# Coefficients of a gated linear recurrence from Ln, Exp and one Newton step, on 512 columns, in place of a Sqrt and a reciprocal on 256

## The chip, the cores and the metric

The kernel runs on one core of a Trainium2 chip. The metric is the device time in microseconds (us) of one execution. Before the change it is 1085.87 us, the median of three runs (1085.77 to 1085.95). Five engines work side by side, each through its own queue of instructions in a fixed order, and wait for each other through semaphores: PE (matrix products; its weight loads are listed apart as PEld), DVE (VectorE), ACT (ScalarE), POOL (GpSimd) and SP, which here only issues transfers.

## The reference, cut to what matters

One decoder layer for 256 tokens of width 2048 in float32: a normalisation, one combined projection into six groups of 1024 channels, two parallel groups of heads, an output projection, and a gated feed-forward part with 5632 hidden channels. The change concerns group A, the gated recurrence (RG-LRU) over 1024 channels:

```python
r = sigmoid(einsum(u_blocks, wa) + ba)
i = sigmoid(einsum(u_blocks, wx) + bx)
log_a = LRU_C * r * log_sigmoid(lam)          # LRU_C = 8
a = exp(log_a)
b = sqrt(-expm1(2.0 * log_a)) * (i * u)
h[t] = a[t] * h[t-1] + b[t]                   # a scan over the 256 tokens
y_lru = h * gelu(lru_gate)
```

With t = tanh(-log_a / 2) both coefficients are rational in t and its root: a = (1 - t) / (1 + t), and sqrt(1 - a*a) = 2 sqrt(t) / (1 + t).

## The kernel before, in words

**Layout.** In the first part activations lie with channels on the 128 partitions and tokens along the free dimension; 256 tokens of one block of 128 channels are a tile of 128x256, and two blocks share one tile of 128x512. The eight blocks of the recurrence are n = 0 to 7, so the lists `tt` (t), `iu` (i times u), `root` and `hs` (the scan's result) hold four tiles of 128x512 each, and `pair(lst, n, name)` is the half that belongs to block n.

**Weights.** All weights stream from memory in loads of 128x1024 (512 KB) into one of six `raw` buffers, issued by SP in the order of the program. Each load is split into a high and a low part, so that products in the faster 32-bit format keep their accuracy: `split` casts `wh<-raw` on ACT (L112) and subtracts `wl<-raw,wh` on DVE (L113). There are four `wh` and four `wl` buffers. A cast for load M therefore waits until PE has read load M-4 for the last time, and PE can run at most three loads ahead of what ACT and DVE are doing now.

**The program.** It is a list of steps; each step is a unit of weights with its matrix products (`fm_tile` for tiles with channels on the partitions, `tm_block` for tiles with tokens there). A step of `fm_tile` uses one unit of two loads: for each pair of weight blocks two products with `wh` (L184, 512 columns) and two with `wl` (L186, 256 columns). The casts and subtractions of a load are written into the program three loads ahead of the step that uses them. Work on ACT, DVE and POOL that follows a product is deferred by a number of steps (`defer`). From this program a scheduler with a model of time of its own makes the final order in each engine's queue, so the queues need not follow the text, and a change of one stage may shift the order around it.

**The stages.** v (first half) to 29 us; the projections lx of the recurrence, then k and q (24 steps of `fm_tile`), to about 169 us; v (second half) and ret_gate (`tm_block`), with the heads of the retention between; lg, the recurrence's output gate, to about 292 us; then the output projection and the feed-forward part to the end.

**The recurrence.** `lru_in` (convolution) and `lru_gate` follow the lx steps. `lru_gate(n)` runs two sigmoids and a tanh on ACT (L372, L373, L375), a lower bound on t on DVE (L376), and i times u on POOL (L377). All eight gates done, `lru_roots` takes four square roots of 128x512 on ACT (L384), which needs another table of functions (an ACT_TABLE_LOAD). Then eight times `lru_scan(n)`: seven DVE operations on 128x256 (L390 to L397), one of them a reciprocal (L391), one square on ACT (L394), and the scan itself on DVE (L398). They are deferred by 12 to 28 steps and so lie among the k, q, v and ret_gate steps, whose casts, subtractions and copies use the same queues. The results `hs` are first read in the lg stage, by `lru_out`.

Of the kernel before, what the change touches and what calls it, by code (L numbers as in the profile page):

```python
# [8 lines left out]
F32 = mybir.dt.float32  # L9
F32R = mybir.dt.float32r  # L10
AF = mybir.ActivationFunctionType
ALU = mybir.AluOpType
PSUM = bass.MemoryType.PSUM

P = 128
D = 2048
S = 256
# [3 lines left out]
NLRU = 8  # L21
NH = 8
EPS = 1e-6
TINY = 1e-30


C_LN1, C_LN2, C_CW, C_CB, C_BA, C_BX, C_LAM, C_GN = 0, 16, 32, 64, 72, 80, 88, 96
# [17 lines left out]
def tile_hymba_layer(ctx: ExitStack, tc: tile.TileContext, A: dict, out: bass.AP):  # L45
    nc = tc.nc
    v, act, pool, pe = nc.vector, nc.scalar, nc.gpsimd, nc.tensor

    cpool = ctx.enter_context(tc.tile_pool(name="consts", bufs=1))
# [13 lines left out]
    def nm(s):  # L63
        counter[0] += 1
        return f"{s}_{counter[0]}"

    def act_tile(name, dt=F32):
        return apool.tile([P, 512], dt, tag="act", name=nm(name))
# [7 lines left out]
    def tmp(name):  # L76
        return tpool.tile([P, S], F32, tag="tmp", name=nm(name))
# [4 lines left out]
    def aux(name):  # L82
        return paux.tile([P, 512], F32, tag="aux", name=nm(name))
# [11 lines left out]
    ones = cpool.tile([P, P], F32, name="ones")  # L95
    eps_t = cpool.tile([P, 1], F32, name="eps_t")
    v.memset(ones, 1.0)
    v.memset(eps_t, EPS)
    warm = cpool.tile([P, 1], F32, name="warm")
    act.activation(out=warm, in_=eps_t, func=AF.Tanh)  # L100

# [5 lines left out]
    def col(c):  # L107
        return small[:, c : c + 1]
# [42 lines left out]
    def mm_fm1(ps, wh, wl, hl, first, last):  # L151

        pe.matmul(ps, wh, hl[:, :S], start=first, stop=False)
        pe.matmul(ps, wh, hl[:, S:], start=False, stop=False)
        pe.matmul(ps, wl, hl[:, :S], start=False, stop=last)
# [17 lines left out]
    def fm_tile(unit, acts, order, post, room=bank):  # L173


        def run():
            ps = room("fm")
            for n in range(0, len(order), 2):
                if n == 8 and halfway:
                    halfway.pop()()  # L180

                two = [(*unit.part(k, P, 0, P), acts[k]) for k in order[n : n + 2]]
                for i, (wh, _, hl) in enumerate(two):
                    pe.matmul(ps, wh, hl, start=n + i == 0, stop=False)  # L184
                for i, (_, wl, hl) in enumerate(two):
                    pe.matmul(ps[:, :S], wl, hl[:, :S], start=False, stop=n + i == len(order) - 1)  # L186
            post(ps)

        program.append(([unit], run))

    def tm_block(units, acts, post, together=1, split=()):


# [36 lines left out]
    def defer(steps, f):  # L230
        later.append([steps, f])
# [73 lines left out]
    c2 = cpool.tile([P, NLRU], F32, name="c2")  # L305
    xcs = [None] * NLRU
    xc = [None] * 4
    tt = [None] * 4
    iu = [None] * 4
    hs = [None] * 4  # L310

    def pair(lst, n, name):
        if lst[n // 2] is None:
            lst[n // 2] = act_tile(name)
        return lst[n // 2][:, (n % 2) * S : (n % 2) * S + S]
# [34 lines left out]
    def lru_in(n, ps):  # L350
        xe = epool.tile([P, 260], F32, tag="xe", name=nm("xe"))
        pool.memset(xe[:, 0:3], 0.0)
        t = tmp("lx")
        halves(ps, t)
        v.tensor_tensor(out=xe[:, 3 : 3 + S], in0=t, in1=r1, op=ALU.mult)
        c = pair(xc, n, "xc")
        act.activation(out=c, in_=xe[:, 0:S], func=AF.Identity, scale=col(C_CW + n), bias=col(C_CB + n))
        for tap in range(1, 4):
            v.scalar_tensor_tensor(
                out=c, in0=xe[:, tap : tap + S], scalar=col(C_CW + 8 * tap + n), in1=c, op0=ALU.mult, op1=ALU.add  # L360
            )
        xcs[n] = act_tile("xcs", F32R)
        split(xcs[n][:, :S], xcs[n][:, S:], c)

    def lru_gate(n):
        c = pair(xc, n, "xc")
        ps = aux("gate")
        for g in range(2):
            wh, wl = (w[:, (n % 2) * 256 + g * P : (n % 2) * 256 + g * P + P] for w in gw[n // 2])
            mm_fm1(ps[:, g * S : g * S + S], wh, wl, xcs[n], True, True)  # L370
        r, i = tmp("r"), tmp("i")
        act.activation(out=r, in_=ps[:, :S], func=AF.Sigmoid, bias=col(C_BA + n))  # L372
        act.activation(out=i, in_=ps[:, S:], func=AF.Sigmoid, bias=col(C_BX + n))  # L373
        t = pair(tt, n, "tt")
        act.activation(out=t, in_=r, func=AF.Tanh, scale=c2[:, n : n + 1])  # L375
        v.tensor_scalar(out=t, in0=t, scalar1=TINY, scalar2=None, op0=ALU.max)  # L376
        pool.tensor_tensor(out=pair(iu, n, "iu"), in0=i, in1=c, op=ALU.mult)  # L377

    root = [None] * 4

    def lru_roots():
        for i in range(4):
            root[i] = act_tile("root")
            act.activation(out=root[i], in_=tt[i], func=AF.Sqrt)  # L384

    def lru_scan(n):

        t, s = pair(tt, n, "tt"), pair(root, n, "root")
        p, a, b = tmp("p"), tmp("a"), tmp("b")
        v.scalar_tensor_tensor(out=p, in0=t, scalar=1.0, in1=s, op0=ALU.add, op1=ALU.mult)  # L390
        v.reciprocal(out=p, in_=p)  # L391
        v.scalar_tensor_tensor(out=a, in0=t, scalar=1.0, in1=s, op0=ALU.subtract, op1=ALU.mult)
        v.scalar_tensor_tensor(out=a, in0=a, scalar=-1.0, in1=p, op0=ALU.mult, op1=ALU.mult)
        act.activation(out=b, in_=s, func=AF.Square)  # L394
        v.tensor_tensor(out=b, in0=b, in1=t, op=ALU.add)
        v.tensor_tensor(out=b, in0=b, in1=p, op=ALU.mult)
        v.tensor_tensor(out=b, in0=b, in1=pair(iu, n, "iu"), op=ALU.mult)  # L397
        v.tensor_tensor_scan(out=pair(hs, n, "hs"), data0=a, data1=b, initial=0.0, op0=ALU.mult, op1=ALU.add)  # L398

    y, yf = [None] * (KT // 2), [None] * (KT // 2)  # L400

# [619 lines left out]
    for n in range(NLRU):  # L1021

        def post(ps, n=n):
            defer(max(1, 4 - n), lambda: lru_in(n, ps))
            defer(max(9, 12 - n), lambda: lru_gate(n))
            if n == NLRU - 1:
                defer(10, lru_roots)
                for m in range(NLRU):
                    defer((12, 15, 18, 20, 22, 24, 26, 28)[m], lambda m=m: lru_scan(m))

        fm_tile(Unit(A["w_lx"][n]), u, range(KT), post, room=aux if n in (2, 3, 6, 7) else bank)

# [169 lines left out]
```

## Time and profile before

| | |
|---|---|
| median of three runs | 1085.87 us |
| the profiled execution: its span, first to last instruction | 1084.4 us |
| PE busy | 1074.2 us (99% of the span) |
| DVE busy | 953.5 us (88%) |
| ACT busy | 660.9 us (61%) |
| POOL busy | 51.0 us (5%) |
| granted clock of TensorE | 0.999 |

The profile records the span only; the runs' time is 1.5 us longer, which lies outside the first and the last instruction. Busy shares are averages over stages with different limits, and a busy PE is not by that alone a PE at its peak. What matters for a change of ACT and DVE work is how far these two run ahead of PE in the stage concerned.

### The profile page before, as it was taken

The page shows a single profiled execution, that of the slowest core. Times are in us where ns is not written, and L with a number is a line of the kernel's source. Part 1 is how long each engine was busy: PE and PEld are TensorE (multiplying, and loading weights), DVE is VectorE, ACT ScalarE, POOL GpSimd, SP SyncE. Part 2 cuts the span into 40 slices and gives each one's busy share as a digit, 9 for nine tenths or more (in the row PEclk, how much of TensorE's full clock was granted, in tenths as well). Part 3 has the DMA queues.
Part 4 walks back from the last instruction along what each step waited for, and adds up shares of the span by engine and source line. Part 5 has one row for each costly group of instructions (what it writes and reads, how often), then busy time and mean ns, then how long its engine had stood idle before and what let it go on. Part 6 is the DMA issues. An engine that isn't in the chain of part 4 may idle for free.

```text
span 1084.4 us, 14584 instructions
## 1 busy us (share of the span) xinstructions
PE 1074.2 (99%) x5101; PEld 899.5 (83%) x5101; DVE 953.5 (88%) x1371; ACT 660.9 (61%) x935; POOL 51.0 (5%) x61
## 2 busy tenths in 40 slices
PE   9999999999999999999999999999999999999997
PEld 7888888888888788888888888888888888888885
DVE  7789799988878889888998998999899899898986
ACT  7666644468746676565566566556556666655563
POOL 0612230000000000000000000000000000000001
PEclk9999999999999999999999999999999999999999
DMA  9964474444565567577677677686675756465652
GB/s 330 333 211 168 160 252 173 174 175 171 181 230 205 184 228 275 198 248 266 220 245 261 220 264 235 233 289 214 233 271 194 265 181 213 171 214 199 212 209 85
DMA packets 69274, 238.32 MB, mean 220 GB/s; under 512 B 7888, under 2 KB 8272, under 8 KB 69200
## 3 DMA queue, kind: packets, MB, share of 16 engines
q1 hardware_dynamic: 68400, 235.29, 62.7%
q0 software_dynamic: 512, 1.57, 0.4%
q8 instruction: 40, 0.66, 0.2%
q10 hardware_dynamic: 288, 0.52, 0.1%
q14 instruction: 34, 0.28, 0.1%
HBM read 235.26 MB, written 2.10 MB: 219 GB/s over the span
## 4 chain that ended last, share of the span: by engine, by line
PE 97%; DVE 1%; issue 1%; DMA 0%; ACT 0%; POOL 0%; SPq 0%; POOLq 0%; ACTq 0%
PE c L670 22%; PE c L672 22%; PE c L671 22%; PE fm L184 11%; PE fm L186 5%; PE tm L164 3%; PE tm L165 3%; PE tm L166 3%; PE p L672 1%; PE p L671 1%; PE p L670 1%; PE ft L833 1%; DMA raw<-in_w_v 0%; PE ht L576 0%; PE sc L482 0%
## 5 line engine op out<-in xcount | busy, mean ns | idle before, releaser
L112 ACT CAST wh<-raw 128x1024 fp32r<-128x1024 f32 (+1 forms) x490 | 460.9, 965 | 362.6 <-PE c L672 132.5
L113 DVE TENSOR_TENSOR wl<-raw,wh 128x1024 fp32r<-128x1024 f32 (+1 forms) x490 | 538.2, 1122 | 91.2 <-ACT wh L112 88.4
L671 PE MATMUL c<-wl,ah 128*128 128x512 f32 x850 | 331.0, 390 | 0.0
L672 PE MATMUL c<-wh,al 128*128 128x512 f32 x850 | 330.4, 389 | 0.0
L670 PE MATMUL c<-wh,ah 128*128 128x512 f32 x850 | 275.0, 391 | 0.2 <-ACT wh L112 0.2
L670 PEld LDWEIGHTS c<-wh,ah 128*128 128x128 f32 x850 | 159.4, 188 | 33.4 <-ACT wh L112 1.1
L672 PEld LDWEIGHTS c<-wh,al 128*128 128x128 f32 x850 | 159.6, 188 | 33.0
L671 PEld LDWEIGHTS c<-wl,ah 128*128 128x128 f32 x850 | 159.6, 188 | 32.7
L184 PE MATMUL fm<-u,wh 128*128 128x512 f32 x512 | 161.3, 396 | 0.0
L186 PEld LDWEIGHTS fm<-u,wl 128*128 128x128 f32 x512 | 96.0, 188 | 22.5
L186 PE MATMUL fm<-u,wl 128*128 128x256 f32 x512 | 101.1, 278 | 0.0
L184 PEld LDWEIGHTS fm<-u,wh 128*128 128x128 f32 x512 | 78.4, 189 | 0.3
L648 DVE TENSOR_TENSOR raw<-raw,raw 128x512 f32<-128x512 f32 x106 | 73.1, 690 | 2.8
L648 DVE TENSOR_TENSOR raw<-raw 128x512 f32<-128x512 f32 x106 | 72.7, 689 | 2.4
L671 PE MATMUL c<-wl,sh 128*128 128x512 f32 x176 | 68.5, 389 | 0.0
L672 PE MATMUL c<-wh,sl 128*128 128x512 f32 x176 | 68.0, 389 | 0.0
L670 PE MATMUL c<-wh,sh 128*128 128x512 f32 x176 | 60.4, 394 | 0.3 <-ACT sh L112 0.3
L165 PE MATMUL tm<-wl,u 128*128 128x512 f32 x128 | 48.8, 394 | 0.0
L166 PE MATMUL tm<-wh,u 128*128 128x512 f32 x128 | 48.7, 390 | 0.0
L164 PE MATMUL tm<-wh,u 128*128 128x512 f32 x128 | 47.3, 398 | 0.8 <-ACT u L288 0.8
L954 POOL TENSOR_TENSOR htok<-htok,fw 128x512 f32<-128x512 f32 x2 | 2.5, 1273 | 895.9 <-ACT junk L947 895.9
L670 PEld LDWEIGHTS c<-wh,sh 128*128 128x128 f32 x176 | 33.1, 188 | 7.3 <-ACT sh L112 0.7
(245 smaller groups left out, 1034.9 us busy)
## 6 DMA issues: line engine op xcount, KB each, us to landing
raw<-in_w_gu SPq DMA_DIRECT2D x212, 512.0 KB, 5.5
raw<-in_w_down SPq DMA_DIRECT2D x91, 512.0 KB, 4.3
raw<-in_w_out SPq DMA_DIRECT2D x34, 512.0 KB, 3.7
raw<-in_w_lx SPq DMA_DIRECT2D x16, 512.0 KB, 6.3
raw<-in_w_k SPq DMA_DIRECT2D x16, 512.0 KB, 3.5
raw<-in_w_q SPq DMA_DIRECT2D x16, 512.0 KB, 4.0
raw<-in_w_rg SPq DMA_DIRECT2D x16, 512.0 KB, 3.4
raw<-in_w_lg SPq DMA_DIRECT2D x16, 512.0 KB, 3.4
```

The source lines that it names most:

```text
L112: act.copy(out=dst_h, in_=src)
L113: v.tensor_tensor(out=dst_l, in0=src, in1=dst_h.bitcast(F32), op=ALU.subtract)
L164: pe.matmul(ps, ah, wh, start=first, stop=False)
L165: pe.matmul(ps, ah, wl, start=False, stop=False)
L166: pe.matmul(ps, al, wh, start=False, stop=last)
L184: pe.matmul(ps, wh, hl, start=n + i == 0, stop=False)
L186: pe.matmul(ps[:, :S], wl, hl[:, :S], start=False, stop=n + i == len(order) - 1)
L648: v.tensor_tensor(out=dst, in0=a, in1=b, op=ALU.add)
L670: pe.matmul(p, ah, bh, start=first, stop=False, skip_group_check=onto)
L671: pe.matmul(p, ah, bl, start=False, stop=False, skip_group_check=onto)
L672: pe.matmul(p, al, bh, start=False, stop=last, skip_group_check=onto)
L833: pe.transpose(pt[:, o : o + P], g[:, (2 * b + c) * P : (2 * b + c) * P + P], ident)
```

## The change

`lru_gate` no longer bounds t from below on DVE, and i times u moves from POOL to DVE. `lru_roots` computes, for each of the four pairs, two first guesses on ACT: Ln of (t + 2^-60) and Exp of -0.5 times that for 1/sqrt(t), and Ln of (t + 1) and Exp of minus that for 1/(1 + t). These are 16 activations on 128x512 instead of four. `lru_scan` now works on a pair at once: seven DVE operations on 128x512 and two copies with scale and bias on ACT give one Newton step for each guess and the two coefficients, and two scans of 128x256 follow. There are four such scans instead of eight, deferred by 12, 16, 20 and 24 steps. No reciprocal and no square is left in it. Matrix products, transfers and their numbers stay as they are.

```diff
-TINY = 1e-30
+TINY = 2.0**-60
...
+    tiny_t = cpool.tile([P, 1], F32, name="tiny_t")
+    v.memset(tiny_t, TINY)
...
-        t = pair(tt, n, "tt")
-        act.activation(out=t, in_=r, func=AF.Tanh, scale=c2[:, n : n + 1])
-        v.tensor_scalar(out=t, in0=t, scalar1=TINY, scalar2=None, op0=ALU.max)
-        pool.tensor_tensor(out=pair(iu, n, "iu"), in0=i, in1=c, op=ALU.mult)
-
-    root = [None] * 4
+        act.activation(out=pair(tt, n, "tt"), in_=r, func=AF.Tanh, scale=c2[:, n : n + 1])
+        v.tensor_tensor(out=pair(iu, n, "iu"), in0=i, in1=c, op=ALU.mult)
+
+    root, inv = [None] * 4, [None] * 4
 
     def lru_roots():
-        for i in range(4):
-            root[i] = act_tile("root")
-            act.activation(out=root[i], in_=tt[i], func=AF.Sqrt)
-
-    def lru_scan(n):
-
-        t, s = pair(tt, n, "tt"), pair(root, n, "root")
-        p, a, b = tmp("p"), tmp("a"), tmp("b")
-        v.scalar_tensor_tensor(out=p, in0=t, scalar=1.0, in1=s, op0=ALU.add, op1=ALU.mult)
-        v.reciprocal(out=p, in_=p)
-        v.scalar_tensor_tensor(out=a, in0=t, scalar=1.0, in1=s, op0=ALU.subtract, op1=ALU.mult)
-        v.scalar_tensor_tensor(out=a, in0=a, scalar=-1.0, in1=p, op0=ALU.mult, op1=ALU.mult)
-        act.activation(out=b, in_=s, func=AF.Square)
-        v.tensor_tensor(out=b, in0=b, in1=t, op=ALU.add)
-        v.tensor_tensor(out=b, in0=b, in1=p, op=ALU.mult)
-        v.tensor_tensor(out=b, in0=b, in1=pair(iu, n, "iu"), op=ALU.mult)
-        v.tensor_tensor_scan(out=pair(hs, n, "hs"), data0=a, data1=b, initial=0.0, op0=ALU.mult, op1=ALU.add)
+        for lst, shift, power in ((root, tiny_t, -0.5), (inv, ones[:, :1], -1.0)):
+            for i in range(4):
+                lst[i] = act_tile("guess")
+                act.activation(out=lst[i], in_=tt[i], func=AF.Ln, bias=shift)
+                act.activation(out=lst[i], in_=lst[i], func=AF.Exp, scale=power)
+
+    def lru_scan(i):
+
+        t, s, p = tt[i], root[i], inv[i]
+        a, e = act_tile("a"), act_tile("e")
+        v.scalar_tensor_tensor(out=e, in0=t, scalar=1.0, in1=p, op0=ALU.add, op1=ALU.mult)
+        v.tensor_tensor(out=t, in0=t, in1=s, op=ALU.mult)
+        v.scalar_tensor_tensor(out=p, in0=e, scalar=2.0, in1=p, op0=ALU.subtract, op1=ALU.mult)
+        v.tensor_tensor(out=s, in0=t, in1=s, op=ALU.mult)
+        act.activation(out=a, in_=p, func=AF.Copy, scale=-2.0, bias=-1.0)
+        act.activation(out=s, in_=s, func=AF.Copy, scale=-0.5, bias=1.5)
+        v.scalar_tensor_tensor(out=p, in0=p, scalar=-2.0, in1=iu[i], op0=ALU.mult, op1=ALU.mult)
+        v.tensor_tensor(out=t, in0=t, in1=s, op=ALU.mult)
+        v.tensor_tensor(out=p, in0=p, in1=t, op=ALU.mult)
+        hs[i] = act_tile("hs")
+        for c in range(2):
+            cs = slice(c * S, c * S + S)
+            v.tensor_tensor_scan(
+                out=hs[i][:, cs], data0=a[:, cs], data1=p[:, cs], initial=0.0, op0=ALU.mult, op1=ALU.add
+            )
...
-                for m in range(NLRU):
-                    defer((12, 15, 18, 20, 22, 24, 26, 28)[m], lambda m=m: lru_scan(m))
+                for i in range(4):
+                    defer((12, 16, 20, 24)[i], lambda i=i: lru_scan(i))
```

The change moves instructions in the queues. The first place is ACT's queue in the k and q stage, from the last tanh of `lru_gate` on. In these rows `wh`, `raw` and `wl` are the parts of a weight load, `fm` a product's result that is copied out as `qk`, `tt` is t, and `guess` a first guess. Before:

```order
L375 ACTIVATE tt_1416<-r_1487,c_112 128x256
L384 ACT_TABLE_LOAD
L384 ACTIVATE root_1542<-tt_1171 128x512
L384 ACTIVATE root_1544<-tt_1201 128x512
L384 ACTIVATE root_1546<-tt_1279 128x512
L112 CAST wh_1551<-raw_1550 128x1024
L170 COPY qk_1539<-fm_1506 128x256
L384 ACTIVATE root_1548<-tt_1416 128x512
L112 CAST wh_1557<-raw_1556 128x1024
```

The same place in the changed kernel, whose lines lie two further down (L114 is the cast, L172 the copy, L385 Ln and L386 Exp); the rows that are left out are six more Ln and, further on, two more Exp:

```order
L376 ACTIVATE tt_1412<-r_1482,c_114 128x256
L385 ACT_TABLE_LOAD
L385 ACTIVATE guess_1536<-tt_1173,tiny_t 128x512
...
L385 ACTIVATE guess_1557<-tt_1412,ones 128x512
L386 ACT_TABLE_LOAD
L386 ACTIVATE guess_1536<-guess_1536 128x512
L114 CAST wh_1561<-raw_1560 128x1024
L172 COPY qk_1533<-fm_1500 128x256
L386 ACTIVATE guess_1539<-guess_1539 128x512
...
L386 ACTIVATE guess_1548<-guess_1548 128x512
L114 CAST wh_1567<-raw_1566 128x1024
```

Between the tanh and the next cast of a weight load there stood one table load and three activations; now there stand two table loads and nine activations. Between that cast and the one after it there stood a copy and one activation, now a copy and four. Three more Exp stand ahead of the third cast (wh_1620).

The second place is DVE's queue beside it. Before:

```order
L113 TENSOR_TENSOR wl_1502<-raw_1500,wh_1501 128x1024
L463 TENSOR_TENSOR rope_1469<-qk_1402,m_1470 64x256 x2
L376 TENSOR_SCALAR tt_1416<-tt_1416 128x256
L113 TENSOR_TENSOR wl_1552<-raw_1550,wh_1551 128x1024
L171 TENSOR_TENSOR qk_1539<-fm_1506,qk_1539 128x256
L113 TENSOR_TENSOR wl_1558<-raw_1556,wh_1557 128x1024
L113 TENSOR_TENSOR wl_1611<-raw_1609,wh_1610 128x1024
```

In the changed kernel:

```order
L115 TENSOR_TENSOR wl_1496<-raw_1494,wh_1495 128x1024
L471 TENSOR_TENSOR rope_1464<-qk_1398,m_1465 64x256 x2
L115 TENSOR_TENSOR wl_1562<-raw_1560,wh_1561 128x1024
L173 TENSOR_TENSOR qk_1533<-fm_1500,qk_1533 128x256
L115 TENSOR_TENSOR wl_1568<-raw_1566,wh_1567 128x1024
L115 TENSOR_TENSOR wl_1621<-raw_1619,wh_1620 128x1024
```

Only the lower bound on t is gone; each subtraction `wl` still waits for its cast. The third place is ACT's queue at the last scan of the changed kernel, among the retention's heads (L396 and L397 are the two copies of `lru_scan`, L505 copies a head's result):

```order
L114 CAST wh_2265<-raw_2264 128x1024
L396 ACTIVATE a_2299<-guess_1557 128x512
L114 CAST wh_2326<-raw_2325 128x1024
L397 ACTIVATE guess_1545<-guess_1545 128x512
L505 COPY o_2195<-pv_2313 128x128
```

The second copy of a scan stands behind a cast that waits for a buffer from PE, and DVE's queue holds the rest of that scan behind the copy. The order of the matrix products is the same in both kernels up to the end of the q stage; between there and the output projection the heads and transposes stand at other places among the same main products, and from the output projection on PE's queue is the same.

## The prediction

> **What bounds the kernel now.** I read the page's shares first, then the chain that ended last, then what PE waited for, then the stretches in which the changed instructions lie.
>
> ```profile
> PE 1074.2 (99%) x5101; PEld 899.5 (83%) x5101; DVE 953.5 (88%) x1371; ACT 660.9 (61%) x935; POOL 51.0 (5%) x61
> PE 97%; DVE 1%; issue 1%; DMA 0%; ACT 0%; POOL 0%; SPq 0%; POOLq 0%; ACTq 0%
> ...
> PE warm L105 <- DVE eps_t L98: 1.1, 1, 1.1
> PE tm L164 <- ACT u L288: 0.8, 2, 0.5
> PE c L670 <- ACT sh L112: 0.3, 1, 0.3
> PE c L670 <- ACT wh L112: 0.2, 1, 0.2
> ...
> 96.00:146.00 50.00, 50.00 (x303) 44.35 (x302) 40.71 (x60) 32.95 (x55) 17.54 (x24) 1.00 0.53 179
> 146.00:182.00 36.00, 36.00 (x192) 30.83 (x191) 35.62 (x56) 16.09 (x21) 6.06 (x6) 1.00 0.58 204
> 182.00:250.00 68.00, 68.00 (x341) 57.78 (x340) 61.50 (x119) 38.19 (x61) 0.00 (x0) 1.00 0.50 177
> 250.00:310.00 60.00, 60.00 (x327) 51.73 (x326) 51.64 (x96) 45.44 (x79) 0.00 (x0) 1.00 0.54 188
> ```
>
> PE carries 97% of the chain, and all its waits come to 2.4 us. In the four stretches from 96 to 310 us, where every changed instruction lies, PE is busy for the whole of each (the second number; DVE is the fourth, ACT the fifth, the granted clock stands before the DMA share). So work taken off DVE, ACT or POOL there gives PE nothing: there is no wait to remove. The change can only matter by making PE wait. How close it comes to that is a question of how far ACT and DVE run ahead of PE, and the closest place is the block of activations at 129 us.
>
> **The change part by part.** First the sums of work, from the groups of instructions (busy us, then mean ns of one).
>
> ```profile
> L391 DVE RECIPROCAL p<-p 128x256 f32<-128x256 f32 x8 | 13.9, 1742 | 0.0
> L392 DVE SCALAR_TENSOR_TENSOR a<-tt,root 128x256 f32<-128x256 f32 x8 | 3.9, 483 | 0.0
> L396 DVE TENSOR_TENSOR b<-b,p 128x256 f32<-128x256 f32 x8 | 3.2, 400 | 0.0
> L398 DVE TENSOR_TENSOR_SCAN hs<-a,b 128x256 f32<-128x256 f32 x8 | 6.3, 796 | 0.0
> L376 DVE TENSOR_SCALAR tt<-tt 128x256 f32<-128x256 f32 x8 | 3.7, 477 | 0.7 <-ACT tt L375 0.6
> L377 POOL TENSOR_TENSOR iu<-i,xc 128x256 f32<-128x256 f32 x8 | 7.5, 945 | 7.1 <-ACT i L373 7.1
> L475 DVE SCALAR_TENSOR_TENSOR sg<-sg,rg 128x512 f32<-128x512 f32 x4 | 2.8, 689 | 2.6 <-ACT sg L474 2.6
> L171 DVE TENSOR_TENSOR qk<-fm,qk 128x256 f32<-128x256 f32 x16 | 6.6, 413 | 0.0
> L394 ACT ACTIVATE b<-root 128x256 f32<-128x256 f32 x8 | 3.3, 417 | 5.9 <-DVE hs L398 4.1 <-DVE rope L464 1.7
> L375 ACT ACTIVATE tt<-r,c 128x256 f32<-128x256 f32 x8 | 4.0, 519 | 0.0
> L417 ACT ACTIVATE q<-q 128x256 f32<-128x256 f32 x8 | 3.3, 416 | 0.7 <-DVE q L416 0.6
> L384 ACT ACTIVATE root<-tt 128x512 f32<-128x512 f32 x4 | 2.3, 624 | 0.0
> L384 ACT ACT_TABLE_LOAD x1 | 1.3, 1283 | 0.0
> ```
>
> DVE loses eight reciprocals (13.9 us), eight times six operations of 400 to 483 ns (the two extremes are shown; about 20 us), eight bounds on t (3.7 us) and keeps eight scans of the same size. It gains 4 x 7 operations on 512 columns at 689 ns (19.3 us) and eight products i times u, like L171 at 413 ns (3.3 us). That is about 15 us less of 189.5 us in the four stretches. POOL loses 7.5 us. ACT loses four roots, one table load and eight squares of about 0.42 us, 7.2 us, and gains 8 Ln, 8 Exp, 8 copies on 512 columns and two table loads, about 18 us. All of it lies beside PE, which does the same products; so the term of DVE and POOL is nothing, for either sign, as long as no weight load arrives late.
>
> The term that is not nothing is the order on ACT. These are ACT, DVE and PE in time (start, duration):
>
> ```profile
> 127.42 1.05 ACT L112 CAST wh<-raw 128x1024 fp32r<-128x1024 f32 x1 [1.44 <-PE fm L184]
> 128.38 0.50 ACT L375 ACTIVATE tt<-r,c 128x256 f32<-128x256 f32 x1
> 128.90 1.28 ACT L384 ACT_TABLE_LOAD   x1
> 130.19 1.67 ACT L384 ACTIVATE root<-tt 128x512 f32<-128x512 f32 x3
> 131.77 1.04 ACT L112 CAST wh<-raw 128x1024 fp32r<-128x1024 f32 x1
> 132.71 0.36 ACT L170 COPY qk<-fm 128x256 f32<-128x256 f32 x1
> 132.97 0.63 ACT L384 ACTIVATE root<-tt 128x512 f32<-128x512 f32 x1
> 133.50 1.04 ACT L112 CAST wh<-raw 128x1024 fp32r<-128x1024 f32 x1
> 135.78 1.05 ACT L112 CAST wh<-raw 128x1024 fp32r<-128x1024 f32 x1 [1.24 <-PE fm L184]
> ...
> 132.84 1.23 DVE L113 TENSOR_TENSOR wl<-raw,wh 128x1024 fp32r<-128x1024 f32 x1 [0.32 <-ACT wh L112]
> ...
> 138.60 0.63 PE L184 MATMUL fm<-u,wh 128*128 128x512 f32 x2
> 141.39 0.63 PE L184 MATMUL fm<-u,wh 128*128 128x512 f32 x2
> ...
> 138.84 0.42 PEld L186 LDWEIGHTS fm<-u,wl 128*128 128x128 f32 x2
> 141.62 0.42 PEld L186 LDWEIGHTS fm<-u,wl 128*128 128x128 f32 x2
> ...
> L482 PE MATMUL sc<-rope,rope x16: 377/379/382, 183.3 to 248.2; 128*128 128x256 f32 x16
> ```
>
> Call the load whose cast starts at 127.42 N. The cast at 135.78 is that of N+3 and was released by PE: PE had read the load four before it, N-1, for the last time. PE therefore begins N at 135.8, N+1 at 138.60 and N+2 at 141.39, 2.79 us each; the rows of PE and PEld show those starts, and that the first weights from `wl` are wanted at 138.84 and 141.62. In the kernel before, `wl` of N+1 is ready at 134.07 (132.84 + 1.23), 4.8 us early. That is the cover the new block uses up.
>
> Nothing of the change lies on ACT before 128.90, so I start there. The table load ends at 130.19. An Ln takes its added constant from a tile of one column; the two tanh groups above differ in just that, a scale from a tile or a number, 519 against 416 ns. So Ln = 624 + 103 = 727 ns. Activations in a row overlap: three roots from 130.19 to 131.77 make 0.527 each, 0.097 less than 624. A step of Ln is then 0.63 us and eight take 7 x 0.63 + 0.73 = 5.14 us, to 135.33. The tanh shows that a load waits for the end of what is before it (128.38 + 0.50, then 0.02): second load 135.35 to 136.63. One Exp at 0.53 us: the cast of N+1 starts at 137.16, not 131.77, and ends at 138.21. DVE holds nothing but that subtraction by then; it starts 0.03 us later, as at 132.84, and ends at 139.47. Wanted at 138.84: **PE waits 0.63 us**. The high part itself is in time.
>
> From 137.16 on: 0.94 us to the copy (131.77 to 132.71), 0.26 us for it, four Exp at 0.527: the cast of N+2 starts at 140.47 and ends at 141.52, its subtraction at 142.78. Wanted at 141.62 + 0.63 = 142.25: **0.53 us more**. Then three Exp: cast N+3 starts at 142.99, `wl` is ready at 145.30, wanted at 138.84 + 2 x 2.79 + 1.16 = 145.58: in time. The next cast has only a copy before it, and the lead grows again. PE never makes up a wait, so the sum is 1.16 us.
>
> Bounds. If Ln steps like the roots (0.527), the cast of N+1 starts at 136.33, its `wl` is in time, and that of N+2 is ready at 141.97 against 141.62: 0.35 us. If nothing on ACT overlaps (0.75 for Ln, 0.64 for Exp), N+1 comes 0.96 us later than in the sum and N+2 loses another 0.5: 2.5 us. Below nothing is excluded here, because PE has no idle time in 96 to 146 us. I take 1.16, since both the surcharge and the overlap are seen in rows of this engine.
>
> The Trainium skill, "ScalarE: Activation LUTs", section "What ACT_TABLE_LOAD costs", gives every function the same time per element, so it has no term for Ln being slower than a root. Its section "Table sets: the hidden batching unit" says that Ln and Exp share one set and need one load; the queue shown above holds two, and with one the whole wait would vanish (1085.9 us).
>
> The other new waits are covered. i times u on DVE waits for a sigmoid, which ends before the tanh that the old bound on t waited for, and sits at the same places. POOL's eight products leave its queue; what stands behind them, rotary products and eight transfers, moves with DVE's addition behind the late copy, some 5 to 6 us, and the transferred tables are first needed by the heads' scores (L482, last row), at 183 us. In a scan, DVE's product with the second ACT copy waits behind a cast, and that cast waits for PE: behind it stand the next `wl` and, at the last scan, the product of a head's scores. From a buffer's release to PE's need lie three loads, 8.4 us; on the way are a cast of 1.05, an activation of 0.6, an operation of 0.69 and a `wl` of 1.23 us, with a few small ones: 3 to 4 us are left. Not hidden, each of four scans would cost what is missing there.
>
> So the span is 1084.4 + 1.2 = 1085.6 us; the runs lie 1.5 us above the span, 1085.87 against 1084.4, and give **1087.0 us**.
>
> **The rivals.**
> (a) The block is hidden after all (1085.9 us): the overlap is larger or the order's first cast earlier than the sum has it. For it: the sum misses by only 0.6 us per load. Against it: the queue is fixed, and the block's length is made of measured rows.
> (b) Slower: ACT's block is longer than the rows of other functions make it. If Ln and Exp ran like a 1024-column cast (steps of 0.95, from 131.77 and 132.71), the first cast comes 3.0 us later, the second 1.7, the third 1.3, and PE waits 3.6 + 2.2 + 1.0: 1085.87 + 6.8 = 1092.7 us. Every microsecond added ahead of the first cast is one on PE, so this decides from about 1 us more than the sum. Against it: tanh, square and root differ little at equal size. The same mechanism with dearer table loads: the Trainium skill, same section on ACT_TABLE_LOAD, counts 2.7 us with the drain, where the row has 1283 ns and 0.02 us of gap; by it the time would be 1.4 us twice later, 1089.9 us.
> (c) The scans' coupling of ACT and DVE is not covered, 1 us at each of four scans: 1091 us. For it: two engines wait for each other and for PE. Against it: the 3 to 4 us.
> (d) Faster: DVE's 15 us matter. They would have to end a wait, and the four rows list 2.4 us, none in these stretches; even the 0.5 us on L112 later on would leave 1085.4 us, no faster than can be told.
>
> **How the numbers follow.** The forecast with its bounds (0.35 to 2.5 us) has 0.62, (a) 0.19, (b) 0.11, (c) 0.04, (d) or another gain 0.04. About 0.2%, 2.2 us here, is what a measurement of this kernel can tell from no change. Slower by more are (b), (c) without their mildest cases and the top of the forecast's own bounds, 0.14; faster by more at most 0.03; within it the rest, 0.83. The range runs from a little under (a) to the upper bound: 1085.5 to 1088.6 us.
>
> **What would show it.** PE or PEld of L186 (now L188) waiting for DVE `wl` at about 139 and 142 us, together near 1.2 us, and the stretch 96 to 146 us with some 49 us of PE; a cast that starts near 137.2 us; two table loads of 1283 ns; Ln near 727 and Exp near 624 ns; DVE some 15 us less busy, with no gain from it. It would be wrong if PE waited elsewhere between 146 and 310 us, if a load cost over 2 us, or if PE's stretch stayed full.

## The result, and the profile after

The changed kernel takes 1087.89 us (median of 18 runs, 1087.40 to 1089.98) and the kernel before, on the same chip, 1085.90 us (18 runs). The ratio is 1.0021, with a 95% interval of 1.0014 to 1.0028: about 2.0 to 2.3 us more. The profiled execution has a span of 1086.7 us, where that of the kernel before has 1084.4.

Busy times and the chain that ended last, from the page of the changed kernel:

```profile
PE 1075.3 (99%) x5101; PEld 898.8 (83%) x5101; DVE 940.1 (87%) x1344; ACT 667.7 (61%) x947; POOL 46.0 (4%) x53
PE 93%; DVE 3%; ACT 2%; issue 1%; DMA 0%; POOL 0%; SPq 0%; POOLq 0%; ACTq 0%
```

DVE lost 13.4 us of work and PE did the same products, and yet the chain now runs over DVE for 3% instead of 1%, and over ACT for 2%. What PE waited for (total, times, longest):

```profile
...
PE tm L167 <- DVE wl L115: 0.5, 1, 0.5
PE c L678 <- ACT wh L114: 0.4, 2, 0.2
PE fm L188 <- DVE wl L115: 0.4, 2, 0.2
```

`fm` L188 and `tm` L167 waiting for a `wl` are new; `c` L678 waits twice for a `wh` instead of once. The stretches that the prediction looked at (length, PE, PEld, DVE, ACT, POOL busy; clock, DMA share, GB/s):

```profile
96.00:146.00 50.00, 49.59 (x298) 43.34 (x297) 32.01 (x50) 39.50 (x66) 4.93 (x7) 1.00 0.43 144
146.00:182.00 36.00, 36.00 (x194) 30.90 (x192) 35.74 (x53) 16.11 (x23) 14.80 (x16) 1.00 0.67 235
182.00:250.00 68.00, 67.51 (x337) 56.90 (x336) 55.84 (x103) 40.53 (x65) 0.00 (x0) 1.00 0.53 175
```

PE is no longer full in the first and in the third. DVE does 8.7 us less in the first and is as full in the second as it was before. The block on ACT, and DVE and PE behind it, in order of time (start, duration):

```profile
128.62 1.28 ACT L385 ACT_TABLE_LOAD   x1
129.92 2.57 ACT L385 ACTIVATE guess<-tt,tiny_t 128x512 f32<-128x512 f32 x4
132.39 2.55 ACT L385 ACTIVATE guess<-tt,ones 128x512 f32<-128x512 f32 x4
134.96 1.28 ACT L386 ACT_TABLE_LOAD   x1
136.26 0.63 ACT L386 ACTIVATE guess<-guess 128x512 f32<-128x512 f32 x1
136.79 1.03 ACT L114 CAST wh<-raw 128x1024 fp32r<-128x1024 f32 x1
...
137.99 2.19 ACT L386 ACTIVATE guess<-guess 128x512 f32<-128x512 f32 x4
140.09 1.03 ACT L114 CAST wh<-raw 128x1024 fp32r<-128x1024 f32 x1
...
137.86 1.23 DVE L115 TENSOR_TENSOR wl<-raw,wh 128x1024 fp32r<-128x1024 f32 x1 [6.22 <-ACT wh L114]
141.15 1.23 DVE L115 TENSOR_TENSOR wl<-raw,wh 128x1024 fp32r<-128x1024 f32 x1 [1.73 <-ACT wh L114]
...
139.14 0.30 PEld L188 LDWEIGHTS fm<-u,wl 128*128 128x128 f32 x2 [0.62 <-DVE wl L115]
142.43 0.30 PEld L188 LDWEIGHTS fm<-u,wl 128*128 128x128 f32 x2 [0.66 <-DVE wl L115]
190.12 0.19 PEld L167 LDWEIGHTS tm<-wl,u 128*128 128x128 f32 x1 [0.91 <-DVE wl L115]
```

DVE stands idle for 6.22 us before the first late subtraction and 1.73 us before the second; PE's weight loads wait 0.62 and 0.66 us. The third wait, 0.91 us, comes 48 us later, in the other form of step.

What each wait cost is read from the starts of one product in both kernels, because PE does the same products and makes up nothing. (Their order is not quite the same through the k and q stage, as was written above: at 145.33 us the changed kernel has two more products with `wh` ahead of the first two with `wl`, and from 148.13 us on the order is again that of the kernel before.) Of the kernel before, then of the changed one: the first product of a gate after 100 us, the first of the second half of v, and the first of the output projection.

```profile
105.07 0.28 PE L153 MATMUL gate<-xcs,gh 128*128 128x256 f32 x1
169.25 0.40 PE L164 MATMUL tm<-wh,u 128*128 128x512 f32 x1
291.72 0.40 PE L670 MATMUL c<-wh,ah 128*128 128x512 f32 x1
```

```profile
104.79 0.28 PE L155 MATMUL gate<-xcs,gh 128*128 128x256 f32 x1
169.96 0.40 PE L166 MATMUL tm<-wh,u 128*128 128x512 f32 x1
293.36 0.40 PE L678 MATMUL c<-wh,ah 128*128 128x512 f32 x1
```

From gate to v it is 0.99 us more (0.71 + 0.28), from v to the output projection 0.93 us more (1.64 - 0.71). Together 1.92 us lie between the gates and the output projection, and below "loss" means this sum. The other thing that sets these two profiles apart is PE waiting at 382 us for a cast whose load landed late: 0.44 us, by the starts of one product. That is chance, as a second profile of each kernel shows: the kernel before has the wait there once too, and the changed one once not.

> The kernel before once more, for a second profile. If the wait of PE for a cast at about 382 us (0.2 us of PE rows, 0.5 us of delay in the changed kernel, none in the first profile of before) is a matter of when transfers land, it can appear here too or not; if it belongs to the change, it is absent.

Measured: one time of 1087.28 us, span 1085.5, loss 0.01. PE and ACT in this profile:

```profile
381.88 0.50 PE L670 MATMUL c<-wh,ah 128*128 128x512 f32 x1 [0.90 <-ACT wh L112]
...
380.78 1.04 ACT L112 CAST wh<-raw 128x1024 fp32r<-128x1024 f32 x1 [2.56 <-DMA raw<-in_w_gu]
```

> The changed kernel once more, for a second profile. The waits at 139, 142 and 190 us come from fixed queues and should return with the same sizes (1.0 and 0.9 us of delay); the one at 382 us may change.

Measured: 1087.88 us, span 1086.0, loss 1.92. The waits at 139, 142 and 190 us are there again, and none at 382. So the difference of 2.0 us lies in two places: the block (1.0), which was predicted, and 190 us (0.9), which was not.

### The profile page after: what moved, and what is told of

It reads as the page before. It is cut to its first block, busy times and chain, and to the rows that moved or that the text cites. A ratio compares the mean times of both kernels' runs of the same rounds, so it can differ in the third digit from the quotient of the medians.

```text
span 1086.7 us, 14560 instructions
## 1 busy us (share of the span) xinstructions
PE 1075.3 (99%) x5101; PEld 898.8 (83%) x5101; DVE 940.1 (87%) x1344; ACT 667.7 (61%) x947; POOL 46.0 (4%) x53
## 4 chain that ended last, share of the span: by engine, by line
PE 93%; DVE 3%; ACT 2%; issue 1%; DMA 0%; POOL 0%; SPq 0%; POOLq 0%; ACTq 0%
PE c L680 22%; PE c L679 22%; PE c L678 22%; PE fm L186 10%; PE fm L188 5%; PE tm L167 2%; PE tm L166 2%; PE tm L168 2%; DVE wl L115 1%; PE p L680 1%; PE p L679 1%; PE p L678 1%; PE ft L841 1%; ACT wh L114 1%; ACT guess L385 0%
## 5 line engine op out<-in xcount | busy, mean ns | idle before, releaser
L114 ACT CAST wh<-raw 128x1024 fp32r<-128x1024 f32 (+1 forms) x490 | 459.9, 965 | 331.3 <-PE c L680 126.7
L678 PE MATMUL c<-wh,ah 128*128 128x512 f32 x850 | 275.3, 391 | 0.4 <-ACT wh L114 0.4
L678 PEld LDWEIGHTS c<-wh,ah 128*128 128x128 f32 x850 | 159.4, 188 | 34.1 <-ACT wh L114 1.8
L188 PEld LDWEIGHTS fm<-u,wl 128*128 128x128 f32 x512 | 95.7, 188 | 23.5 <-DVE wl L115 1.3
L188 PE MATMUL fm<-u,wl 128*128 128x256 f32 x512 | 101.0, 279 | 0.4 <-DVE wl L115 0.4
L678 PE MATMUL c<-wh,sh 128*128 128x512 f32 x176 | 60.4, 394 | 0.3 <-ACT sh L114 0.3
L167 PE MATMUL tm<-wl,u 128*128 128x512 f32 x128 | 48.8, 393 | 0.5 <-DVE wl L115 0.5
L678 PEld LDWEIGHTS c<-wh,sh 128*128 128x128 f32 x176 | 33.1, 188 | 7.3 <-ACT sh L114 0.7
```

What stands on the lines that cost most here:

```text
L114: act.copy(out=dst_h, in_=src)
L167: pe.matmul(ps, ah, wl, start=False, stop=False)
L678: pe.matmul(p, ah, bh, start=first, stop=False, skip_group_check=onto)
```

## The experiments

Three theories stood for the wait at 190 us. **Leftover**: what DVE and ACT fell behind at the block is still missing there. **Coupling**: the new scans make DVE wait for ACT's two copies and ACT for DVE. **The iu products**: they are 3.3 us more on DVE. The kernels ran on several chips, so each ratio is to the kernel before on the same chip: 1086.56 us for the four runs that come first, 1086.34 for the two after them.

### New scans, old roots

```diff
-                act.activation(out=lst[i], in_=tt[i], func=AF.Ln, bias=shift)
-                act.activation(out=lst[i], in_=lst[i], func=AF.Exp, scale=power)
+            act.activation(out=root[i], in_=tt[i], func=AF.Sqrt)
+            pool.memset(inv[i], 0.6)
```

> The changed kernel with the block of first guesses taken out: four square roots stand in for one guess and a constant (0.6, written by POOL) for the other, so the coefficients are not the reference's; the scans on 512 columns with their two ACT copies stay. Theory 'leftover' (the wait at 190 us is what the late block left behind, because DVE stood idle for 6.2 us and then stays full): no PE wait at 139, 142 or 190 us, 1085.9 us. Rival 'coupling' (the ACT copies wait for DVE with weight casts behind them, whatever the block did): no wait at 139 and 142, but about 0.9 us near 190 us, 1086.8 us.

Measured: 1086.61 us, ratio 1.0001 (0.9993 to 1.0010), loss 0.14 us. No wait at 139, 142 or 190 us. The new scans alone cost nothing, and DVE's lighter work gains nothing either.

### Old scans, new roots

```diff
-            act.activation(out=root[i], in_=tt[i], func=AF.Sqrt)
+                act.activation(out=lst[i], in_=tt[i], func=AF.Ln, bias=shift)
+                act.activation(out=lst[i], in_=lst[i], func=AF.Exp, scale=power)
```

> The kernel before with the changed kernel's 16 activations in place of four square roots; the second set of results is not used; scans, bound and product as before. The queue now holds four table loads: one load, three Ln, one load and one Exp before the first cast (5.1 us), then two Exp, a load and five Ln before the second, a load and two Exp before the third. By the sum of the prediction's prices PE waits nothing at the first cast, about 1.4 us at the second and 0.5 us at the third: 1087.8 us. 'Leftover': a further wait between 150 and 200 us, 1088.5 us or more. 'Coupling': none there, 1087.8 us.

Measured: 1090.99 us, ratio 1.0043 (1.0030 to 1.0055), loss 4.45 us. The scheduler interleaved the groups, so the block has four table loads instead of two; that was foreseen, but both theories had the time too low (1087.8 and 1088.5 us). From gate to v the loss is 2.87 us where 1.9 were expected, and 1.6 us follow behind it. PE waits at 142 to 150 us, and, with the old scans in DVE's queue, at 189.74 us (0.23) and 194.42 us (0.74) for `wl`. The wait near 190 us therefore needs no new scan; with the run above, in which the block was missing, it is the block that it needs.

### One table load

```diff
-                act.activation(out=lst[i], in_=tt[i], func=AF.Ln, bias=shift)
+                act.activation(out=lst[i], in_=tt[i], func=AF.Exp, bias=shift)
```

> The changed kernel with Exp in place of Ln (values are not the reference's): the same 16 activations in the same places, one table load instead of two. The block is 1.28 us shorter ahead of the first cast: by the measured times wl would be ready 0.7 us before it is wanted both times, so no wait at 139 and 142 us, 1.0 us less than the changed kernel. 'Leftover': DVE still idles some 5 us, the wait at 190 us shrinks or goes: 1086.0 to 1086.6 us. 'Coupling': it stays at 0.9 us, 1086.9 us.

Measured: 1087.14 us, ratio 1.0008 (0.9999 to 1.0016), loss 0.50 us. The wait near 190 us shrinks to 0.47 us, as the leftover theory had it; by coupling it would have stayed at 0.9. This is the cleanest of the comparisons: the queues of PE and DVE are the same, instruction for instruction, as in the changed kernel, and ACT's lacks the second load and nothing else. ACT, DVE and PE in this kernel:

```profile
128.82 1.28 ACT L385 ACT_TABLE_LOAD   x1
...
135.56 1.03 ACT L114 CAST wh<-raw 128x1024 fp32r<-128x1024 f32 x1
...
136.63 1.23 DVE L115 TENSOR_TENSOR wl<-raw,wh 128x1024 fp32r<-128x1024 f32 x1 [4.78 <-ACT wh L114]
...
184.01 0.68 DVE L400 TENSOR_TENSOR guess<-guess,tt 128x512 f32<-128x512 f32 x1
...
187.64 1.23 DVE L115 TENSOR_TENSOR wl<-raw,wh 128x1024 fp32r<-128x1024 f32 x1
...
188.92 0.19 PEld L167 LDWEIGHTS tm<-wl,u 128*128 128x128 f32 x1 [0.47 <-DVE wl L115]
```

And DVE in the changed kernel, at the same place in its queue:

```profile
184.09 1.21 DVE L115 TENSOR_TENSOR wl<-raw,wh 128x1024 fp32r<-128x1024 f32 x1
185.22 0.68 DVE L400 TENSOR_TENSOR guess<-guess,tt 128x512 f32<-128x512 f32 x1
185.93 1.28 DVE L404 TENSOR_TENSOR_SCAN hs<-a,guess 128x256 f32<-128x256 f32 x2
187.12 0.39 DVE L471 TENSOR_TENSOR rope<-qk,m 64x256 f32<-64x256 f32 x1
...
188.85 1.23 DVE L115 TENSOR_TENSOR wl<-raw,wh 128x1024 fp32r<-128x1024 f32 x1
```

The first subtraction behind the block is 1.23 us earlier with one load (136.63 against 137.86). The one that is late at 190 us is still 1.21 us earlier (187.64 against 188.85), 50 us further on. From 146 to 202 us DVE is full (55.60 of 56 us in the changed kernel), so the delay passes through its queue undiminished. The wait follows from these rows alone: the subtraction is 1.21 us later in the changed kernel, PE itself 0.77 us later (169.96 against 169.19 at the start of v: its stalls at 139 and 142 us, less the 0.20 us by which the profile with one load is later from the gates on), and 0.47 + 1.21 - 0.77 = 0.91 us, the wait measured. With the shorter block 0.5 us remain at this place and nothing at 139 and 142. One load more costs 1.42 us in all: 0.97 at the block and 0.45 here. The ratios, 1.0021 and 1.0008, are 1.4 us apart as well.

### The two copies on DVE

```diff
-        act.activation(out=a, in_=p, func=AF.Copy, scale=-2.0, bias=-1.0)
-        act.activation(out=s, in_=s, func=AF.Copy, scale=-0.5, bias=1.5)
+        v.tensor_scalar(out=a, in0=p, scalar1=-2.0, scalar2=-1.0, op0=ALU.mult, op1=ALU.add)
+        v.tensor_scalar(out=s, in0=s, scalar1=-0.5, scalar2=1.5, op0=ALU.mult, op1=ALU.add)
```

> The changed kernel with the two copies of each scan as operations with two constants on DVE instead of ACT; nothing of a scan then stands between weight casts on ACT, and DVE has eight operations more. The block is unchanged: 1.0 us at 139 and 142 us by both. 'Coupling': no wait at 190 us, 1087.0 us. 'Leftover': DVE, full from 146 us on, has 3 to 5 us more to do, so the wait stays or grows, 1088 us or more.

Measured: 1088.49 us, ratio 1.0022 (1.0013 to 1.0031), loss 1.92 us. No scan waits for ACT any more, and PE still waits at 139.56 us (0.18), 142.86 us (0.24) and 182.05 us (0.40). The coupling falls.

### The product i times u back on POOL

```diff
-        v.tensor_tensor(out=pair(iu, n, "iu"), in0=i, in1=c, op=ALU.mult)
+        pool.tensor_tensor(out=pair(iu, n, "iu"), in0=i, in1=c, op=ALU.mult)
```

> The changed kernel with the product i times u back on POOL, as before. By the sum it is hidden on either engine, because DVE idles 6 us behind the late cast: the same waits at 139, 142 and 190 us, within 0.3 us of the changed kernel's 1087.9 us. A rival, that the eight products on DVE take part in the wait at 190 us, would have 0.5 us less or more.

Measured: 1088.67 us on a chip that takes 1086.34 us for the kernel before, ratio 1.0021 (1.0012 to 1.0030), loss 1.96 us, with the three waits of the changed kernel at 139.55, 142.85 and 190.56 us. The moved product costs nothing and its place is free.

### The block in four parts

```diff
-                defer(10, lru_roots)
+                for part in range(4):
+                    defer(10 + part, lambda part=part: lru_roots(part))
...
-                    defer((12, 16, 20, 24)[i], lambda i=i: lru_scan(i))
+                    defer((14, 17, 20, 23)[i], lambda i=i: lru_scan(i))
```

> The changed kernel with the same 16 activations written in four groups of four, one step apart, and the scans deferred by 14, 17, 20 and 23 steps; nothing is left out. The queue then holds two smaller blocks, each with two table loads (four in all instead of two), four Ln and an Exp ahead of a cast: 5.6 us instead of 8.2 us, and with a few casts between the two. 'Leftover': the first cast's wl is ready 2 us before PE wants it, no wait at 139 to 150 us and none near 190 us: 1085.9 to 1086.3 us, although ACT does 2.6 us more work. 'Coupling': about 0.9 us stay near 190 us, 1086.8 us. A third view, that ACT's total work is what costs, would have it slower than the changed kernel.

Measured: 1088.26 us, ratio 1.0017 (1.0009 to 1.0026), loss 1.79 us. The expectation that the time would fall to that of the kernel before was missed. PE's two waits in order of time (a weight load waits a third time, 0.50 us at 188.31 us):

```profile
174.91 0.50 PE L167 MATMUL tm<-wl,u 128*128 128x512 f32 x1 [0.37 <-DVE wl L115]
183.63 0.50 PE L167 MATMUL tm<-wl,u 128*128 128x512 f32 x1 [0.25 <-DVE wl L115]
```

Three stretches of this kernel (DVE is the fourth number), then the same three of the kernel before:

```profile
128.00:138.00 10.00, 10.00 (x59) 8.71 (x59) 4.94 (x10) 9.94 (x15) 0.00 (x0) 1.00 0.22 75
138.00:146.00 8.00, 8.00 (x48) 6.98 (x47) 7.27 (x11) 7.19 (x10) 5.28 (x8) 1.00 0.80 268
146.00:158.00 12.00, 12.00 (x70) 10.45 (x69) 8.06 (x13) 9.34 (x13) 3.77 (x5) 1.00 0.80 289
```

```profile
128.00:138.00 10.00, 10.00 (x60) 8.76 (x59) 8.32 (x12) 7.83 (x12) 1.01 (x2) 1.00 0.50 167
138.00:146.00 8.00, 8.00 (x47) 6.97 (x46) 6.96 (x13) 3.85 (x5) 5.90 (x10) 1.00 0.76 241
146.00:158.00 12.00, 12.00 (x71) 10.45 (x70) 11.88 (x19) 4.85 (x6) 2.46 (x2) 1.00 0.70 253
```

At 139 and 142 us nothing waits now, so spreading does what it should at the block. But there are four table loads, the scans come later, and DVE stands idle for 9.7 us of the 30 from 128 to 158 us, where it was idle for 2.8 in the kernel before. The whole loss has moved to the steps of v. Ahead of the first of these subtractions stand a scan's end and a rotation again (170.60 to 173.63 us). A version that is faster than both kernels did not come out of this.

### Is it enough that DVE is late?

The obvious reading was a debt: DVE is full from 146 to 202 us, so idle time before that can't be worked off, whatever made it. The other reading, in the expectations "the new scans' order", was that it depends on how the changed scans stand in the queues. Three kernels put sums of 128x512 (0.676 us each, nobody reads them) into the kernel before, after the old roots, and leave ACT as it was.

```diff
+    def more():
+        for _ in range(1):
+            v.tensor_reduce(out=spare, in_=tt[3], axis=mybir.AxisListType.X, op=ALU.add)
...
+                for step in range(10, 14):
+                    defer(step, more)
```

Four sums so; eight and twelve with two and three of them a step.

> The kernel before with four more sums over 128x512 on VectorE (0.6 to 0.7 us each, 2.4 to 2.8 us in all), put between 130 and 145 us, and nothing changed on ScalarE. Two theories of PE's wait at 190 us in the changed kernel. 'DVE's debt': what VectorE loses by standing idle at 128 to 146 us cannot be worked off in the full stretch from 146 to 202 us, whatever made it idle, and PE waits once the debt is larger than the lead of the subtraction that is wanted at 188.5 us, 1.5 us in the kernel before. 'The new scans' order': the wait comes from how the changed scans stand in the queues. By the debt: VectorE was idle 2.7 us in that stretch, the four fill it, no PE wait, time of the kernel before, ratio 1.000 (0.9992 to 1.0008). By the order: the same, 1.000.

Measured: 1086.59 us against 1086.35 for the kernel before on that chip, ratio 1.0003 (0.9994 to 1.0012), loss 0.02 us.

> The kernel before with eight such sums on VectorE between 130 and 155 us (4.8 to 5.6 us in all), ScalarE unchanged. By 'DVE's debt': 2.7 us of it fall into idle time, 2.1 to 2.9 us remain, 0.6 to 1.4 us more than the lead of 1.5 us at 188.5 us: PE waits for the low part of weights between 175 and 200 us, 0.6 to 1.4 us in all, and the time is 0.6 to 1.4 us above the kernel before, ratio 1.0006 to 1.0013. By 'the new scans' order': no wait there, ratio 1.000, since the old scans stand where they stood.

Measured: 1086.68 us, ratio 1.0003 (0.9994 to 1.0012), loss -0.03 us. The subtraction that starts at 185.74 us in the kernel before started at 187.71, and PE did not wait. The expectation had its lead too small. The two rows of the kernel before that give it, the subtraction and the first weight load that reads it:

```profile
185.74 1.21 DVE L113 TENSOR_TENSOR wl<-raw,wh 128x1024 fp32r<-128x1024 f32 x1
...
189.68 0.19 PEld L165 LDWEIGHTS tm<-wl,u 128*128 128x128 f32 x1
```

It is ready at 186.95 and wanted at 189.68: 2.7 us, not 1.5. In the changed kernel it is ready at 190.08 (188.85 + 1.23) and wanted at 189.21 (190.12 - 0.91): 3.1 us later on DVE, and wanted 0.5 us earlier, since PE, though 0.7 us late, has the first scores of a head (0.8 us) and a little more behind these products and no longer ahead of them.

> The kernel before with twelve sums over 128x512 on VectorE between 130 and 155 us, ScalarE's work unchanged. With eight, the subtraction that starts at 185.74 us in the kernel before started at 187.71, 1.97 us late and 35 us after the last sum, and PE did not wait: the weights it makes are wanted at 189.68 and were ready at 186.95, a lead of 2.7 us and not the 1.5 that the expectations of the first two such runs took. 'DVE's debt': four more sums of 0.68 us make it 4.7 us late, 2.0 us more than the lead; PE waits for low parts of weights somewhere between 160 and 200 us, 1.5 to 2.3 us in all; time 1.5 to 2.3 us above the kernel before, ratio 1.0014 to 1.0021. 'The new scans' order': a late VectorE alone costs nothing here; no PE wait, ratio 1.0000 to 1.0006.

Measured: 1086.06 us against 1085.97, ratio 1.0003 (0.9993 to 1.0012), loss 0.13 us. Missed: the time did not rise by 1.5 to 2.3 us. With 8.1 us of sums, of which at most 2.7 found idle time, the subtraction in question was only 1.2 us late (186.96 against 185.74), because the scheduler, which had the sums in its program, had made another order. The subtraction after it was 3.2 us late (190.37 against 187.21), and there a weight load did wait:

```profile
191.63 0.19 PEld L165 LDWEIGHTS tm<-wl,u 128*128 128x128 f32 x1 [0.28 <-DVE wl L113]
```

So the debt in this form falls: DVE's queue between 146 and 202 us holds work that can wait, and idle time lost does not by itself reach PE. What counts is how late the one subtraction is that PE wants, against its lead, and the order in the queue sets both. What more than twelve sums would cost, no run shows.

### Less for DVE to do in the changed kernel

```diff
-            v.tensor_tensor(out=a, in0=a, in1=cr, op=ALU.mult)
-            v.tensor_tensor(out=b, in0=b, in1=cr, op=ALU.mult)
```

> The changed kernel without the products with the cosine of the rotation of q and k (two of 0.41 us for each of eight pairs; so q and k are not rotated rightly, and the heads' values are not the reference's). It takes about 3.3 us off VectorE between 146 and 188 us and leaves ScalarE's block of logarithms as it is. By 'DVE's debt': the waits at 139 and 142 us stay (1.0 us), the wait at 190 us (0.9 us) is gone; span 1085.4 to 1085.8, ratio to the kernel before 1.0007 to 1.0013, and 1.0 us less than the changed kernel. By 'the new scans' order': the wait at 190 us stays, since the scan there still stands ahead of the subtraction that is late; ratio 1.0016 to 1.0022.

Measured: 1088.97 us, ratio 1.0025 (1.0014 to 1.0036), loss 2.63 us. The waits at the block are as before (loss 0.97); the other moved and grew, although DVE had less to do:

```profile
186.10 0.50 PE L167 MATMUL tm<-wl,u 128*128 128x512 f32 x1 [1.09 <-DVE wl L115]
...
181.19 0.68 DVE L400 TENSOR_TENSOR guess<-guess,tt 128x512 f32<-128x512 f32 x1
181.90 1.28 DVE L404 TENSOR_TENSOR_SCAN hs<-a,guess 128x256 f32<-128x256 f32 x2
183.09 0.39 DVE L469 TENSOR_TENSOR rope<-qk,m 64x256 f32<-64x256 f32 x1
...
184.82 1.23 DVE L115 TENSOR_TENSOR wl<-raw,wh 128x1024 fp32r<-128x1024 f32 x1
```

It is the same group as in the changed kernel that stands ahead of the late subtraction: the end of a scan and the four sums of a rotation, 3.6 us. The scheduler had made another order, with this scan earlier. Both theories failed here: the debt, which wanted the wait gone, and the plain form of the other one, which wanted it unchanged.

**What follows.** A delay at the block reaches 190 us undiminished when the queue is the same (one table load against two). It costs PE something where the queue holds several us of other work ahead of a subtraction that is wanted: in the changed kernel a scan's end and a rotation, with the old scans two reciprocals (189.60 to 193.20 us). Extra work that the scheduler knows of moves the order and costs next to nothing (0.13 us with twelve sums). That the queues of PE and DVE do not differ at all between one load and two shows that the scheduler's order did not react to 1.28 us of loading. That its clock simply runs behind the chip in the block, and that the order would have been a good one at the times it expected, is argued from this and not shown. Open is also why the order of the four-part block came out so that it loses as much.

## Why the prediction was right, and where it was not

The time was forecast at 1087.0 us, in a range of 1085.5 to 1088.6, and "within 0.2%" (2.2 us) as the likeliest outcome. 1087.89 us lies in the range, and the change lies on the edge of the 0.2%: 2.0 us by the medians, 2.3 by the ratio. The mechanism at the block was right, but that the time stayed in the range was in part luck: the upper bound was room for longer rows on ACT (and 1085.87 + 2.5 is 1088.4, not 1088.6), and what filled it was a wait at another place that the sum did not have. Point by point:

- **PE bounds all four stretches, so work taken from DVE and POOL gains nothing.** Right. With the new scans alone the ratio was 1.0001. Rival (d) is out. The sums of work were rough: DVE lost 13.4 us where 15 were forecast, POOL 5.0 and not 7.5 (its rotary products grew from 957 to 1186 and from 788 to 990 ns; the cause is open), and ACT gained 6.8 us, not some 11. None of it decided anything.
- **The prices.** Right to a few hundredths: a load 1283 ns; a step of Ln 2.47 / 4 = 0.62 us (132.39 - 129.92), against 0.63; Exp and Ln as in these groups of the changed kernel (mean ns last but one):

```profile
L386 ACT ACTIVATE guess<-guess 128x512 f32<-128x512 f32 x8 | 4.5, 623 | 0.0
L385 ACT ACTIVATE guess<-tt,tiny_t 128x512 f32<-128x512 f32 x4 | 2.6, 716 | 0.0
L385 ACT ACTIVATE guess<-tt,ones 128x512 f32<-128x512 f32 x4 | 2.6, 712 | 0.0
```

  Forecast were 624 and 727. The 0.09 us between Ln and Exp are the surcharge for the column operand, as read from the two tanh groups, and not one for Ln: in the kernel with one table load, where Exp stands in its place, it is there too, against 624 ns without the operand.

```profile
L385 ACT ACTIVATE guess<-tt,tiny_t 128x512 f32<-128x512 f32 x4 | 2.6, 714 | 0.0
```

  The Trainium skill, "ScalarE: Activation LUTs", section "What ACT_TABLE_LOAD costs", counts the same time per element for every function, and about 93 ns more for each operand of one column; these rows agree with both. So it does have the term that the prediction says it lacks. Its 2.7 us for a switch are 1283 ns of load, as in the row, and about 1380 ns of drain; the drain does not show here, where the load starts 0.02 us after the end of the last Ln (132.39 + 2.55, then 134.96) and the Exp 0.02 us after the load.
- **The casts at 137.16 and 140.47 us, PE waiting 0.63 and 0.53 us.** Right. The whole stage runs 0.28 us earlier in this profile; with that added the casts start at 137.07 and 140.37. PE lost 0.99 us there, against 1.16. Rivals (a) and (b), the hidden and the longer block, are out.
- **"The lead grows again", and for the scans "3 to 4 us are left".** This is the step that failed, and the prediction had named the sign of it: PE waiting elsewhere between 146 and 310 us. The third load behind the block was in time, as said. The cover of three loads is what ACT and DVE can be ahead of PE (not PE ahead of them, as written further up), and the lead of the later ones was reckoned from durations on the way from a buffer's release to PE's need, as if these operations stood alone in their queues. DVE is full from 146 to 202 us; the subtraction at 188.85 us had had its cast 5 us before and stood behind a scan and a rotation. That term is 0.93 us and was missing from the sum, whose 1.16 us became 0.99 at the block and 0.93 here, 1.92 together. Rival (c) had the scans in it, but at four places, by the coupling with ACT and at 1 us each; it was one place, without the coupling.
- **One table or two.** The Trainium skill, same page, section "Table sets: the hidden batching unit", has Ln and Exp in one set. The queue had two loads, as the prediction saw, and the runs give the price of the second one: 1.42 us of PE's time of the 1.92.
- **1.5 us outside the span.** In the changed kernel's runs it was 1.8 to 1.9 us. The medians differ by 1.99 us and the loss is 1.92, so this term hardly matters for the difference.

## What to carry to other kernels

Where an engine off the critical path is busy without a gap for tens of microseconds, a delay at the start of that stretch can still be there at its end; here it was, with the same order in the queue. Check the lead of each operand of the bounding engine through the whole full stretch, by the rows of that queue, and not only at the block that was lengthened. A mean of durations says nothing there; what stands ahead of the one operand that is wanted does. And compare the position of one product in both traces at three or four places before explaining a difference of spans, because it tells a cost of the change from a transfer that landed late by chance.

## What was not expected of the hardware

- A second table load in the middle of a group costs more than its row: with it the first cast starts 1.43 us later after the same start of the block (136.79 - 128.62 against 135.56 - 128.82), 0.15 us more than 1.28. Neighbouring activations overlap here by about 0.1 us (a step of Ln is 0.62 us, one Ln 0.716), while the load starts 0.02 us after the end of the last Ln and the Exp 0.02 us after the load.
- The landing of one weight load at 380 us differs from one execution to the next, in either kernel: PE waited 0.22 us for it in the changed kernel's profile and not at all in its second, not at all in that of the kernel before and 0.90 us in its second, and 1.1 us with one table load. That is more than half of the effect that was to be explained.
- Waits that show as 0.19 and 0.23 us on PE cost it 0.99 us in starts: the weight loads' waits of 0.62 and 0.66 us were nearer.
